# Whole-load squares and sums, one root per store, and paired adds for the last loads in an Lp-pool kernel

## The chip, the cores and the metric

One core of one Trainium2 chip. The metric is the device time of one execution in microseconds (us); profiles are of one execution each. ACT (ScalarE) and DVE (VectorE) are the two engines that compute here; DMA engines move the data, and SPq and ACTq in the profiles are the two queues on which transfers are issued. A transfer "lands" when its last byte is in place.

## The reference

Pooling over windows of four neighbours with p = 2: the root of the mean of squares.

```python
x: (32, 256, 4096) float32;  p = 2.0;  kernel_size = 4
for i in range(1024):
    window = np.abs(x[:, :, 4*i:4*i+4]) ** p
    result[:, :, i] = np.mean(window, axis=-1) ** (1.0 / p)
```

It reads 134.2 MB and writes 33.6 MB, and each input is used once.

## The kernel before

The input is taken as one flat array, cut into 22 loads: 18 of 128 x 13184, then four smaller. Three input slots rotate; results of two loads ("group") gather in one output tile and leave with one store. A load is worked on in pieces (`chunks`): ACT squares the piece in place, DVE sums each four neighbours, ACT takes the root of the piece before it.

```python
    W, O_W = 13184, 6592
    X_SLOTS, O_SLOTS = 3, 2
    slots = [[(W, [4416, 4384, 4384])]] * 18
    slots += [[(6592, [3296, 3296])] * 2, [(6592, [3296, 3296]), (5056, [2528, 2528])]]
    groups = [2] * 9 + [3, 1]
    late = {7, 8, 9, 10}          # groups whose store goes out on the load queue, at the end
    in_x = {9, 10}                # groups whose results lie in an input slot
    # ... (pools, addresses)
    def root(g, o, ends):
        nc.scalar.activation(out=o, in_=o, func=Act.Sqrt, scale=1.0 / k)
        if ends and g not in late:
            store(g, nc.scalar)
    # ...
    for i in range(n):
        s, _, w, chunks = loads[i]
        while ahead < n and loads[ahead][0] < s + X_SLOTS:
            load(ahead)           # nc.sync.dma_start; waits until the slot's last sum is done
            ahead += 1
        # ... (output tile of the group)
        for step in chunks:
            v = xs[i][:, c:c + step]
            nc.scalar.activation(out=v, in_=v, func=Act.Square)
            o = ots[g][:, at + c // k:at + (c + step) // k]
            nc.vector.tensor_reduce(out=o, in_=v.rearrange("p (n j) -> p n j", j=k),
                                    axis=mybir.AxisListType.X, op=mybir.AluOpType.add)
            if pending is not None:
                root(*pending)
            c += step
            pending = (g, o, i == firsts[g] + groups[g] - 1 and c == w)
    root(*pending)
    for g in sorted(late):
        store(g, nc.sync)
```

Of the kernel before, what the change touches and what calls it, by code (L numbers as in the profile page):

```python
# [1 line left out]

# [4 lines left out]


@with_exitstack
def kernel(  # L10
    ctx: ExitStack,
    tc: tile.TileContext,
    x: bass.AP,
    p: float,
    kernel_size: int,
    out: bass.AP,
):






    nc = tc.nc

    assert float(p) == 2.0, "kernel specialized for p == 2"
    k = int(kernel_size)
    assert k == 4, "kernel specialized for kernel_size == 4"

    P = nc.NUM_PARTITIONS  # L30
    fp32 = mybir.dt.float32
    Act = mybir.ActivationFunctionType
    xf = x.rearrange("b c l -> (b c l)")
    of = out.rearrange("b c l -> (b c l)")
    total = xf.shape[0] // P

    W, O_W = 13184, 6592
    X_SLOTS, O_SLOTS = 3, 2
    slots = [[(W, [4416, 4384, 4384])]] * 18
    slots += [[(6592, [3296, 3296])] * 2, [(6592, [3296, 3296]), (5056, [2528, 2528])]]  # L40
    groups = [2] * 9 + [3, 1]
    late = {7, 8, 9, 10}
    in_x = {9, 10}


    loads = [(s, sum(w for w, _ in slot[:j]), *slot[j]) for s, slot in enumerate(slots)
             for j in range(len(slot))]
    n = len(loads)
    assert sum(w for _, _, w, _ in loads) == total

    firsts = [sum(groups[:g]) for g in range(len(groups))]
    assert sum(groups) == n
    group_of = [g for g, count in enumerate(groups) for _ in range(count)]
    columns = [sum(w for _, _, w, _ in loads[firsts[g]:firsts[g] + groups[g]])
               for g in range(len(groups))]

    x_pool = ctx.enter_context(tc.tile_pool(name="x_pool", bufs=X_SLOTS))
    o_pool = ctx.enter_context(tc.tile_pool(name="o_pool", bufs=O_SLOTS))
    ctx.enter_context(tc.manual_schedule())

    def block(flat, g, div):
        at, width = sum(columns[:g]) * P // div, columns[g] * P // div
        return flat[at:at + width].rearrange("(p w) -> p w", p=P)

    slot_tiles = {}
    xs = {}

    def load(i):
        s, at, w, _ = loads[i]
        if at == 0:  # L70
            slot_tiles[s] = x_pool.tile([P, W], fp32, name="xt")
        v = slot_tiles[s][:, at:at + w]
        g = group_of[i]
        src = sum(loads[j][2] for j in range(firsts[g], i))
        nc.sync.dma_start(out=v, in_=block(xf, g, 1)[:, src:src + w])  # L75
        xs[i] = v

    ots = {}

    def store(g, queue):  # L80
        queue.dma_start(out=block(of, g, k), in_=ots[g])  # L81

    def root(g, o, ends):
        nc.scalar.activation(out=o, in_=o, func=Act.Sqrt, scale=1.0 / k)  # L84
        if ends and g not in late:
            store(g, nc.scalar)

    ahead = 0
    while ahead < n and loads[ahead][0] < X_SLOTS - 1:
        load(ahead)  # L90
        ahead += 1
    pending = None
    for i in range(n):
        s, _, w, chunks = loads[i]
        while ahead < n and loads[ahead][0] < s + X_SLOTS:
            load(ahead)
            ahead += 1
        g = group_of[i]
        if i == firsts[g]:
            pool, width = (o_pool, O_W) if g not in in_x else (x_pool, W)  # L100
            t = pool.tile([P, width], fp32, name="ot" if g not in in_x else "xt")
            ots[g] = t[:, 0:columns[g] // k]
        at = sum(loads[j][2] for j in range(firsts[g], i)) // k
        assert sum(chunks) == w
        c = 0
        for step in chunks:
            v = xs[i][:, c:c + step]
            nc.scalar.activation(out=v, in_=v, func=Act.Square)  # L108
            o = ots[g][:, at + c // k:at + (c + step) // k]
            nc.vector.tensor_reduce(  # L110
                out=o, in_=v.rearrange("p (n j) -> p n j", j=k),
                axis=mybir.AxisListType.X, op=mybir.AluOpType.add,
            )
            if pending is not None:
                root(*pending)
            c += step
            pending = (g, o, i == firsts[g] + groups[g] - 1 and c == w)
    root(*pending)
    for g in sorted(late):
        store(g, nc.sync)  # L120


# [1 line left out]
_INS = ['x', 'p', 'kernel_size']  # L124
_OUTS = [((32, 256, 1024), 'float32')]

_NUMBERS = {'p': 2.0, 'kernel_size': 4}


# [26 lines left out]
```

## Time and profile before

| | before |
|---|---|
| median of three runs | 394.89 us (394.77 to 394.97) |
| span of the profiled run | 393.0 us |
| moved | 167.8 MB, 427 GB/s over the span |
| busy, DVE and ACT | 282.4 and 292.4 us |

These lines are from the page of the profile: busy time, and then the span in 40 slices of 9.8 us each, a digit being tenths of busy time.

```profile
DVE 282.4 (72%) x62; ACT 292.4 (74%) x126; POOL 0.2 (0%) x4
...
DMA  8999999999999999999999999999999999999997
GB/s 344 429 429 440 429 424 381 443 459 429 413 440 435 429 427 432 429 440 441 437 448 421 432 462 435 392 429 472 429 413 451 425 429 429 424 429 427 438 429 329
```

No engine that computes is near its limit, and the DMA row has a 9 in every slice but the first and the last. That row is the first thing to look at: where it never falls, the time is bytes over rate.

The groups of instructions by shape (line, engine, operation, shapes, count, then busy us and mean ns of one, then the idle time before it):

```profile
L110 DVE TENSOR_REDUCE ot<-xt 128x1096 f32<-128x4384 f32 x36 | 169.9, 4719 | 6.7 <-ACT xt L108 6.4
L108 ACT ACTIVATE xt<-xt 128x4384 f32<-128x4384 f32 x36 | 138.3, 3843 | 2.9 <-ACT ot L84 2.9
...
L84 ACT ACTIVATE ot<-ot 128x1096 f32<-128x1096 f32 x36 | 39.7, 1103 | 1.1 <-DVE ot L110 0.9
```

The DMA issues, with the median time from issue to landing as the last number:

```profile
xt<-in_x_dram SPq DMA_DIRECT2D x18, 6592.0 KB, 39.7
out_dram<-ot ACTq DMA_DIRECT2D x7, 3296.0 KB, 26.4
...
out_dram<-xt SPq DMA_DIRECT2D x1, 632.0 KB, 5.0
```

A load is under way for 39.7 us although it needs 15.6 us alone: it mostly waits in a queue that is never empty. The end of the timeline (start, duration, engine, what):

```profile
381.39 6.11 SPq L81 DMA_DIRECT2D out_dram<-xt  x2
383.47 0.71 ACT L84 ACTIVATE xt<-xt 128x632 f32<-128x632 f32 x1
383.60 2.79 DVE L110 TENSOR_REDUCE xt<-xt 128x632 f32<-128x2528 f32 x1 [0.46 <-ACT xt L108]
386.42 0.73 ACT L84 ACTIVATE xt<-xt 128x632 f32<-128x632 f32 x1 [2.23 <-DVE xt L110]
```

The last root ends at 387.15 us and the last store leaves with it.

### The profile page before, as it was taken

The page shows a single profiled execution, that of the slowest core. Times are in us where ns is not written, and L with a number is a line of the kernel's source. Part 1 is how long each engine was busy: PE and PEld are TensorE (multiplying, and loading weights), DVE is VectorE, ACT ScalarE, POOL GpSimd, SP SyncE. Part 2 cuts the span into 40 slices and gives each one's busy share as a digit, 9 for nine tenths or more (in the row PEclk, how much of TensorE's full clock was granted, in tenths as well). Part 3 has the DMA queues.
Part 4 walks back from the last instruction along what each step waited for, and adds up shares of the span by engine and source line. Part 5 has one row for each costly group of instructions (what it writes and reads, how often), then busy time and mean ns, then how long its engine had stood idle before and what let it go on. Part 6 is the DMA issues. An engine that isn't in the chain of part 4 may idle for free.

```text
span 393.0 us, 316 instructions
## 1 busy us (share of the span) xinstructions
DVE 282.4 (72%) x62; ACT 292.4 (74%) x126; POOL 0.2 (0%) x4
## 2 busy tenths in 40 slices
DVE  0068989494959495949594959595859686899992
ACT  1099986777786768686958695959595949899991
POOL 0000000000000000000000000000000000000000
DMA  8999999999999999999999999999999999999997
GB/s 344 429 429 440 429 424 381 443 459 429 413 440 435 429 427 432 429 440 441 437 448 421 432 462 435 392 429 472 429 413 451 425 429 429 424 429 427 438 429 329
DMA packets 4754, 167.79 MB, mean 427 GB/s; under 512 B 528, under 2 KB 528, under 8 KB 656
## 3 DMA queue, kind: packets, MB, share of 16 engines
q1 hardware_dynamic: 3744, 144.15, 85.3%
q10 hardware_dynamic: 1008, 23.63, 14.0%
q14 instruction: 2, 0.02, 0.0%
HBM read 134.22 MB, written 33.55 MB: 427 GB/s over the span
## 4 chain that ended last, share of the span: by engine, by line
DMA 62%; ACT 19%; DVE 14%; issue 2%; ACTq 0%; SPq 0%
DMA xt<-in_x_dram 62%; ACT xt L108 15%; DVE ot L110 11%; DVE xt L110 3%; ACT ot L84 3%; ACT xt L84 1%; ACTq L81 0%; SPq L75 0%; ACTq L108 0%
## 5 line engine op out<-in xcount | busy, mean ns | idle before, releaser
L110 DVE TENSOR_REDUCE ot<-xt 128x1096 f32<-128x4384 f32 (+1 forms) x54 | 255.4, 4731 | 102.7 <-ACT xt L108 102.4
L108 ACT ACTIVATE xt<-xt 128x4384 f32<-128x4384 f32 (+3 forms) x62 | 230.3, 3716 | 89.2 <-DMA xt<-in_x_dram 86.3
L84 ACT ACTIVATE ot<-ot 128x1096 f32<-128x1096 f32 (+1 forms) x54 | 59.8, 1108 | 1.8 <-DVE ot L110 0.9
L110 DVE TENSOR_REDUCE xt<-xt 128x824 f32<-128x3296 f32 (+1 forms) x8 | 27.0, 3384 | 1.3 <-ACT xt L108 1.2
L84 ACT ACTIVATE xt<-xt 128x824 f32<-128x824 f32 (+1 forms) x8 | 6.7, 841 | 3.0 <-DVE xt L110 2.9
L108 ACT ACT_TABLE_LOAD x1 | 1.3, 1283 | 0.7 <-PEq L137 0.7
L84 ACT ACT_TABLE_LOAD x1 | 1.3, 1283 | 0.0
L137 POOL MEMSET const-bfloat16-1.0<- 128x1 bf16 x1 | 0.1, 101 | 0.0
L137 POOL MEMSET const-uint8-127<- 128x1 uint8 x1 | 0.1, 101 | 0.0
L137 POOL MEMSET const-float32-0.0<- 128x1 f32 x1 | 0.1, 98 | 0.2 <-issue 0.2
L137 POOL MEMSET const-float32-1.0<- 128x1 f32 x1 | 0.1, 98 | 0.0
## 6 DMA issues: line engine op xcount, KB each, us to landing
xt<-in_x_dram SPq DMA_DIRECT2D x18, 6592.0 KB, 39.7
out_dram<-ot ACTq DMA_DIRECT2D x7, 3296.0 KB, 26.4
xt<-in_x_dram SPq DMA_DIRECT2D x3, 3296.0 KB, 24.6
out_dram<-ot SPq DMA_DIRECT2D x2, 3296.0 KB, 29.6
xt<-in_x_dram SPq DMA_DIRECT2D x1, 2528.0 KB, 26.4
out_dram<-xt SPq DMA_DIRECT2D x1, 2472.0 KB, 9.3
out_dram<-xt SPq DMA_DIRECT2D x1, 632.0 KB, 5.0
```

Of the source, the lines that this page charges most:

```text
L84: nc.scalar.activation(out=o, in_=o, func=Act.Sqrt, scale=1.0 / k)
L108: nc.scalar.activation(out=v, in_=v, func=Act.Square)
L110: nc.vector.tensor_reduce(out=o, in_=v.rearrange("p (n j) -> p n j", j=k), axis=mybir.AxisListType.X, op=mybir.AluOpType.add,)
L137: nc = _bacc.Bacc("TRN2", target_bir_lowering=False, num_devices=1)
```

## The change

Its intent is fewer and larger instructions: one square and one sum per 13184-column load, one root per store. For the last loads, where DVE sets the pace, a sum becomes two adds: the first adds columns 0, 1 of each window to columns 2, 3 and packs its results into the front half of the same tile, the second adds the two that remain. Tiles are fixed in place of rotating pools.

```diff
-    slots = [[(W, [4416, 4384, 4384])]] * 18
-    slots += [[(6592, [3296, 3296])] * 2, [(6592, [3296, 3296]), (5056, [2528, 2528])]]
+    slots = [[(W, [W])]] * 16 + [[(W, [6592, 6592])]] * 2
+    slots += [[(6592, [6592]), (6592, [6592])], [(6592, [6592]), (5056, [2528, 2528])]]
-    in_x = {9, 10}
+    in_x = {9: (2, 0), 10: (2, 4944)}
+    FINE, ENDS, LAG = {21}, {19, 20}, 1
+    PAIRS = 17
...
+    x_tiles = [x_pool.tile([P, W], fp32, name=f"xt{j}") for j in range(X_SLOTS)]
+    o_tiles = [o_pool.tile([P, O_W], fp32, name=f"ot{j}") for j in range(O_SLOTS)]
...
+    def total_sum(o, v, i):
+        if i < PAIRS:
+            nc.vector.tensor_reduce(...)          # as before
+            return
+        q = v.rearrange("p (n j) -> p n j", j=k)
+        front = v[:, 0:v.shape[1] // 2]
+        h = front.rearrange("p (n j) -> p n j", j=2)
+        nc.vector.tensor_tensor(out=h, in0=q[:, :, 0:2], in1=q[:, :, 2:4], op=add)
+        nc.vector.tensor_tensor(out=o, in0=h[:, :, 0], in1=h[:, :, 1], op=add)
...
-            if pending is not None:
-                root(*pending)
+            while pending and pending[0][0] <= done - LAG:
+                root(*pending.pop(0)[1:])
...
+            ends = summed == columns[g] // k
+            if ends or i in FINE or (i in ENDS and c == w):
+                pending.append((done - 1, g, ots[g][:, rooted:summed], ends))
+                rooted = summed
```

More of the change, by code (lines that the diff above doesn't have):

```diff
@@ L55 @@
                for g in range(len(groups))]
-    x_pool = ctx.enter_context(tc.tile_pool(name="x_pool", bufs=X_SLOTS))
-    o_pool = ctx.enter_context(tc.tile_pool(name="o_pool", bufs=O_SLOTS))
+    x_pool = ctx.enter_context(tc.tile_pool(name="x_pool", bufs=1))
+    o_pool = ctx.enter_context(tc.tile_pool(name="o_pool", bufs=1))
+    x_tiles = [x_pool.tile([P, W], fp32, name=f"xt{j}") for j in range(X_SLOTS)]
+    o_tiles = [o_pool.tile([P, O_W], fp32, name=f"ot{j}") for j in range(O_SLOTS)]
     ctx.enter_context(tc.manual_schedule())
@@ L63, in block @@
         return flat[at:at + width].rearrange("(p w) -> p w", p=P)
-    slot_tiles = {}
     xs = {}
@@ L69, in load @@
         s, at, w, _ = loads[i]
-        if at == 0:
-            slot_tiles[s] = x_pool.tile([P, W], fp32, name="xt")
-        v = slot_tiles[s][:, at:at + w]
+        v = x_tiles[s % X_SLOTS][:, at:at + w]
         g = group_of[i]
@@ L86, in root @@
             store(g, nc.scalar)
+    def total_sum(o, v, i):
+        add = mybir.AluOpType.add
+        if i < PAIRS:
+            nc.vector.tensor_reduce(
+                out=o, in_=v.rearrange("p (n j) -> p n j", j=k),
+                axis=mybir.AxisListType.X, op=add,
+            )
+            return
[4 more added lines that the diff above has]
+        nc.vector.tensor_tensor(out=o, in0=h[:, :, 0], in1=h[:, :, 1], op=add)
     ahead = 0
@@ L91 @@
         ahead += 1
-    pending = None
+    pending = []
+    done = 0
     for i in range(n):
@@ L99 @@
         if i == firsts[g]:
-            pool, width = (o_pool, O_W) if g not in in_x else (x_pool, W)
-            t = pool.tile([P, width], fp32, name="ot" if g not in in_x else "xt")
-            ots[g] = t[:, 0:columns[g] // k]
-        at = sum(loads[j][2] for j in range(firsts[g], i)) // k
+            t, first = (o_tiles[g % O_SLOTS], 0) if g not in in_x else (x_tiles[in_x[g][0]], in_x[g][1])
+            ots[g] = t[:, first:first + columns[g] // k]
+            summed = rooted = 0
         assert sum(chunks) == w
@@ L108 @@
             nc.scalar.activation(out=v, in_=v, func=Act.Square)
-            o = ots[g][:, at + c // k:at + (c + step) // k]
-            nc.vector.tensor_reduce(
-                out=o, in_=v.rearrange("p (n j) -> p n j", j=k),
-                axis=mybir.AxisListType.X, op=mybir.AluOpType.add,
-            )
-            if pending is not None:
-                root(*pending)
-            c += step
-            pending = (g, o, i == firsts[g] + groups[g] - 1 and c == w)
-    root(*pending)
+            total_sum(ots[g][:, summed:summed + step // k], v, i)
+            while pending and pending[0][0] <= done - LAG:
+                root(*pending.pop(0)[1:])
+            done += 1
+            c += step
+            summed += step // k
+            ends = summed == columns[g] // k
+            if ends or i in FINE or (i in ENDS and c == w):
+                pending.append((done - 1, g, ots[g][:, rooted:summed], ends))
+                rooted = summed
+    for job in pending:
+        root(*job[1:])
     for g in sorted(late):
```

## The prediction

> **What bounds the kernel now.** The DMA engines. In the page's slices the DMA row is 9 from the second slice to the last but one, 427 GB/s over the span. In the chain of waits the same square recurs every 117 us (50.70, 168.26, 285.00 us), in which six loads of 6.75 MB and three stores of 3.375 MB move: 432 GB/s. The Trainium skill ("DMA: Bandwidth & Descriptors", Specifications) gives 435 GB/s as the fabric ceiling; this trace agrees. All 167.8 MB at 432 GB/s take 388.4 us; with some 1.7 us before the first packet and 1.5 us after the last, that is nearly the span of 393.0 us. DVE is busy 72%, ACT 74%. The compute in the chain only frees slots for loads that then wait in the queue (39.7 us from issue to landing, where a load alone takes 15.6 us). Even the last 20 us move 400 to 450 GB/s until 388 us, so the tail's compute hides under stores.
>
> **What the change does.** The same 22 loads and 11 stores, sizes and queues. 62 squares become 25; 62 sums become 18 reductions and 7 pairs of adds; 62 roots become 13. From the groups by shape, a square costs 180 ns + 0.836 ns per column, a reduction 140 + 1.045, a root 200 + 0.825. ACT's busy time falls from 292 to about 283 us. A 6592-column pair of adds should cost 3.6 + 1.9 us against 7.0 for one reduction ("VectorE: DVE Perf Modes", perf-mode tier table: fp32 tensor_tensor at 1×; no run shows it yet); DVE falls from 282 to about 268 us. None of this is on the critical path.
>
> Latency gets worse. A load is squared in 11.2 us, then reduced in 13.9: the slot comes free 25 us after landing, not 18.7. Loads are issued 6 us later; issue to landing shrinks from 39.7 to about 33 us. A load needs 15.7 to 19.5 us of transfer, so 13 us of queue are left and the engines never run dry. Stores on ACT leave about 12 us later (a whole square and a 5.7 us root ahead); a store lands in some 26 us, about 7 us before its output tile is written again.
>
> Tail, worked through with these durations: group 8's root ends near 365 us (before 359), group 9's store leaves near 383 (381.4), the last near 388.5 (387.2). The queue holds group 8's store until about 385 and group 9's until about 390, so a few tenths to one us is lost.
>
> **Prediction.** 395.1 us, range 393.9 to 396.6. Faster by over 2%: 0.005; within 2%: 0.97; slower by over 2%: 0.025.
>
> **What would show it.** DMA row at 9 throughout, 425 to 428 GB/s; ACT instructions from 126 to 40; 13184-column square 11.2 us, reduction 13.9; adds 3.6 and 1.9; load issue to landing 31 to 35 us; last store issued at 388 to 389 us.
>
> **What would make it wrong.** Strided adds at two cycles an element would put over 20 us more DVE work into a tail where DVE is busiest: the last stores come late, and the kernel ends 10 to 20 us later. A store that lands later than 33 us would hold up the sum two groups on. If 13 us of queue were too little for sixteen drifting engines, the rate in the middle would fall below 425 GB/s.

## The result, and the profile after

Ratios here are the mean time of one kernel's fast runs over that of the other's of the same rounds, so not quite the ratio of the medians quoted.

| | before | after |
|---|---|---|
| median of six runs | 394.92 us (394.77 to 395.22) | 395.84 us (395.61 to 396.42) |
| ratio, 95% interval | | 1.0025 (1.0012 to 1.0038) |
| span of the profiled run | 393.0 us | 393.7 us |
| busy, DVE and ACT | 282.4, 292.4 us | 267.8, 281.7 us |
| median us from issue to landing, full load | 39.7 | 31.7 |

The kernel is a quarter of a per cent slower, outside the noise but far below anything that 86 fewer ACT instructions might have suggested. The page of after:

```profile
DVE 267.8 (68%) x32; ACT 281.7 (72%) x40; POOL 0.2 (0%) x4
...
DMA  8999999999999999999899999999999999999996
GB/s 343 429 429 429 434 455 439 386 429 429 434 469 434 442 445 383 431 471 429 386 429 471 429 426 439 421 429 429 429 445 442 426 450 450 402 429 425 438 423 291
```

The same row of nines (one 8 in the middle). ACT and DVE lost 10.7 and 14.6 us of work, and nobody was waiting for it. The groups by shape show what each new instruction costs:

```profile
L93 DVE TENSOR_REDUCE ot<-xt 128x3296 f32<-128x13184 f32 x16 | 222.2, 13886 | 105.1 <-ACT xt L125 105.1
L125 ACT ACTIVATE xt<-xt 128x13184 f32<-128x13184 f32 x16 | 179.0, 11190 | 91.8 <-DMA xt<-in_x_dram 90.1 <-ACT ot L86 1.7
L86 ACT ACTIVATE ot<-ot 128x6592 f32<-128x6592 f32 x9 | 51.2, 5684 | 0.4 <-DVE ot L103 0.4
...
L102 DVE TENSOR_TENSOR xt<-xt 128x3296 f32<-128x3296 f32 x5 | 17.9, 3587 | 6.0 <-ACT xt L125 5.9
L93 DVE TENSOR_REDUCE ot<-xt 128x1648 f32<-128x6592 f32 x2 | 14.0, 7020 | 5.5 <-ACT xt L125 3.7 <-DMA out_dram<-ot 1.9
L103 DVE TENSOR_TENSOR xt<-xt 128x1648 f32<-128x1648 f32 x3 | 5.6, 1875 | 0.1
```

A pair of adds over 6592 columns takes 3.59 + 1.88 = 5.46 us, one reduction of the same 7.02 us. That is what the prediction had put down for adds at full pace, though they read with strides and the first writes into the tile it reads; no run has the same adds without strides. The issues:

```profile
xt<-in_x_dram SPq DMA_DIRECT2D x18, 6592.0 KB, 31.7
out_dram<-ot ACTq DMA_DIRECT2D x7, 3296.0 KB, 27.2
...
out_dram<-xt SPq DMA_DIRECT2D x1, 632.0 KB, 5.9
```

The 8 us between 39.7 and 31.7 have two parts. From the fourth load to the last full one, a load is issued 3.0 to 6.8 us later than before, and it lands between 4.7 us sooner and 0.7 us later than before (the stores, which share the engines, now leave later). So the later issue did not make the loads land late: only the wait in the queue shrank. The end of the timeline:

```profile
381.72 5.65 SPq L83 DMA_DIRECT2D out_dram<-xt  x2
383.80 0.71 ACT L86 ACTIVATE xt<-xt 128x632 f32<-128x632 f32 x1
383.93 1.48 DVE L102 TENSOR_TENSOR xt<-xt 128x1264 f32<-128x1264 f32 x1 [1.61 <-ACT xt L125]
385.44 0.82 DVE L103 TENSOR_TENSOR xt<-xt 128x632 f32<-128x632 f32 x1
386.29 0.73 ACT L86 ACTIVATE xt<-xt 128x632 f32<-128x632 f32 x1 [1.77 <-DVE xt L103]
```

The last root ends at 387.02 us, 0.13 us *earlier* than before, yet the last store lands 5.9 us after its issue, not 5.0. That is the whole of the 0.7 us between the two spans, and it is lost neither by ACT nor by DVE.

It can be traced one step further. Each transfer is done by sixteen DMA engines, and the trace has sixteen landing events for each ("DMA: Bandwidth & Descriptors" in the Trainium skill, section "Why a DMA increments its semaphore by 16 and not by 1", says that each engine's last descriptor counts one; the trace agrees). The sixteen landings of the last load, in us after the first of them, worked out from the trace:

```
before   0.0 0.0 0.0 0.0 0.2 0.2 0.3 0.3 0.3 0.3 0.4 0.4 0.4 0.6 0.8 0.9
after    0.0 0.0 0.1 0.1 0.2 0.2 0.2 0.3 0.3 0.3 0.4 0.5 0.5 0.5 0.6 1.9
```

In after, one engine is 1.3 us behind the fifteenth, and one is still so far behind at the last store: 0.96 us of spread before, 1.98 after. The kernel ends when the last engine does. (A landing does not name its engine; that it is the same one is inferred from the lag, which is 1.3 us in each transfer that lands from 340.4 us on.) The lag arises in the body of the kernel: it is 0.5 us in the first four loads, 0.9 us in the next, which lands at 87.6 us and is the first to share its way with a store, and 1.4 us in the load that lands at 184.7 us.

The packet records of the traces (start, time and size of each packet; no view prints them) tell what the sixteen did on the whole. The packets of loads and stores took 389.8 us per engine in before and 389.6 us in after, and from 5 to 383 us at least sixteen were in flight at over 99% of the moments in both. So the engines of after had no more to do and did not stand idle; the time only fell less evenly on them.

### The profile page after: what moved, and what is told of

It is laid out like the page before. It is cut to its first block, busy times and chain, and to the rows that moved or that the text cites. A ratio compares the mean times of both kernels' runs of the same rounds, so it can differ in the third digit from the quotient of the medians.

```text
span 393.7 us, 192 instructions
## 1 busy us (share of the span) xinstructions
DVE 267.8 (68%) x32; ACT 281.7 (72%) x40; POOL 0.2 (0%) x4
## 2 busy tenths in 40 slices
DMA packets 4752, 167.77 MB, mean 426 GB/s; under 512 B 528, under 2 KB 528, under 8 KB 656
## 3 DMA queue, kind: packets, MB, share of 16 engines
q10 hardware_dynamic: 1008, 23.63, 13.9%
## 4 chain that ended last, share of the span: by engine, by line
DMA 47%; ACT 26%; DVE 19%; issue 6%; SPq 0%; ACTq 0%
DMA xt<-in_x_dram 47%; ACT xt L125 19%; DVE ot L93 14%; ACT ot L86 6%; DVE xt L102 3%; DVE ot L103 1%; DVE xt L103 1%; ACT xt L86 1%; ACT L86 0%; SPq L77 0%; ACTq L83 0%
## 5 line engine op out<-in xcount | busy, mean ns | idle before, releaser
L93 DVE TENSOR_REDUCE ot<-xt 128x3296 f32<-128x13184 f32 (+1 forms) x18 | 236.2, 13123 | 110.6 <-ACT xt L125 108.7
L125 ACT ACTIVATE xt<-xt 128x13184 f32<-128x13184 f32 (+2 forms) x25 | 223.1, 8936 | 102.0 <-DMA xt<-in_x_dram 100.3
L86 ACT ACTIVATE ot<-ot 128x6592 f32<-128x6592 f32 x9 | 51.2, 5684 | 0.4 <-DVE ot L103 0.4
L102 DVE TENSOR_TENSOR xt<-xt 128x3296 f32<-128x3296 f32 (+1 forms) x7 | 20.9, 2983 | 7.6 <-ACT xt L125 7.5
L86 ACT ACTIVATE xt<-xt 128x632 f32<-128x632 f32 (+2 forms) x4 | 6.0, 1492 | 2.2 <-DVE xt L103 2.2
L103 DVE TENSOR_TENSOR xt<-xt 128x1648 f32<-128x1648 f32 (+1 forms) x5 | 7.3, 1452 | 0.2
L103 DVE TENSOR_TENSOR ot<-xt 128x1648 f32<-128x1648 f32 x2 | 3.7, 1874 | 0.1
L125 ACT ACT_TABLE_LOAD x1 | 1.3, 1283 | 0.7 <-PEq L156 0.7
L86 ACT ACT_TABLE_LOAD x1 | 1.3, 1283 | 0.0
## 6 DMA issues: line engine op xcount, KB each, us to landing
xt<-in_x_dram SPq DMA_DIRECT2D x18, 6592.0 KB, 31.7
```

The source lines that it names most:

```text
L102: nc.vector.tensor_tensor(out=h, in0=q[:, :, 0:2], in1=q[:, :, 2:4], op=add)
L103: nc.vector.tensor_tensor(out=o, in0=h[:, :, 0], in1=h[:, :, 1], op=add)
```

## The experiments

All diffs are against after unless it is said otherwise, and are cut to changed lines. Kernels of one call ran on one chip beside before (394.94, 394.94 and 394.84 us in the three calls), and each ratio is to the before of its own call. "Spread" is the time from the first to the last of the sixteen landings of the last load.

### Is compute anywhere on the path? `dma_only`

```diff
+    BIT = 128
+    for t in o_tiles: nc.vector.memset(t, 1.0)
-            v = xs[i][:, c:c + step]
+            v = xs[i][:, c:c + BIT]            # squares, sums and roots likewise: 128 columns, 32 results
```

> Wrong result on purpose: after, but every square, sum and root works on 128 columns (32 results) only; all loads and stores keep their sizes, queues and order. If compute is wholly off the critical path, as predicted: 393.3 to 395 us, at most 0.4% under before, with DVE and ACT busy under 15%. If compute still holds up the DMA anywhere: 391 us or less.

Measured: 395.06 us (394.66 to 395.39), ratio to before 1.0004 (0.9992 to 1.0017), result wrong as intended. That is 0.06 us above the range expected for compute off the path. The page:

```profile
DVE 19.0 (5%) x34; ACT 11.8 (3%) x40; POOL 0.2 (0%) x4
...
DMA  8999999999999999999999999999999999999997
```

With DVE and ACT down from 549.5 us of work together to 30.8, the time is the same within noise. This settles the main question: with these transfers, taking away nearly all of the squares, sums and roots gains nothing that can be measured (the interval reaches 0.08% below before). What the change saved lay beside the critical path.

### Which part brought the 0.9 us? `fixed_only`, `coarse_body`, `coarse_tail`

Two theories stood against each other. A: one of the sixteen DMA engines falls behind in the body (loads 0 to 15), because stores leave later there and mix with loads. B: the loss comes from the new tail (the last six loads). A third cause could be the fixed tiles, so that comes first.

`fixed_only` keeps the fixed tiles and takes back everything else:

```diff
-    slots = [[(W, [W])]] * 16 + [[(W, [6592, 6592])]] * 2
-    slots += [[(6592, [6592]), (6592, [6592])], [(6592, [6592]), (5056, [2528, 2528])]]
+    slots = [[(W, [4416, 4384, 4384])]] * 18
+    slots += [[(6592, [3296, 3296])] * 2, [(6592, [3296, 3296]), (5056, [2528, 2528])]]
-    FINE, ENDS, LAG = {21}, {19, 20}, 1
-    PAIRS = 17
+    FINE, ENDS, LAG = set(range(22)), set(), 1
+    PAIRS = 99
```

> Before's pieces of squares, sums and roots, but the fixed tiles of after. Both theories: same as before, 394.9 us (394.6 to 395.3), because the tiles change neither the order of the DMA nor any size. If it takes 395.6 or more, the 0.9 us of the change comes from the tiles and not from the coarse pieces.

Measured: 394.79 us, ratio 0.9998 (0.9985 to 1.0010). The tiles do nothing.

`coarse_body` has whole-load pieces for loads 0 to 15 and before's pieces and reductions after that:

```diff
-    slots = [[(W, [W])]] * 16 + [[(W, [6592, 6592])]] * 2
-    slots += [[(6592, [6592]), (6592, [6592])], [(6592, [6592]), (5056, [2528, 2528])]]
+    slots = [[(W, [W])]] * 16 + [[(W, [4416, 4384, 4384])]] * 2
+    slots += [[(6592, [3296, 3296])] * 2, [(6592, [3296, 3296]), (5056, [2528, 2528])]]
-    FINE, ENDS, LAG = {21}, {19, 20}, 1
-    PAIRS = 17
+    FINE, ENDS, LAG = set(range(16, 22)), set(), 1
+    PAIRS = 99
```

> After's coarse pieces for loads 0 to 15, before's pieces for the last six loads. Theory A (the 0.9 us is one DMA engine of the sixteen that falls behind the others while late stores and loads interleave in the body; it is still behind at the end): 395.5 to 396.3 us, and the 16 landings of the last store spread over about 2 us, as after, not 1 us as before. Theory B (the 0.9 us comes from the new tail: adds, one long root of group 8, fewer pieces): 394.7 to 395.2 us.

Measured: 396.01 us, ratio 1.0027 (1.0013 to 1.0041). The time hits theory A, but the run is not clean: its last store left only at 389.6 us, so the spread at that store was 0.2 us, not 2; at the last load it was 1.79 us. It needed a repeat with a quicker tail (`body_adds` below).

`coarse_tail` is the other half:

```diff
-    slots = [[(W, [W])]] * 16 + [[(W, [6592, 6592])]] * 2
+    slots = [[(W, [4416, 4384, 4384])]] * 16 + [[(W, [6592, 6592])]] * 2
-    FINE, ENDS, LAG = {21}, {19, 20}, 1
+    FINE, ENDS, LAG = set(range(16)) | {21}, {19, 20}, 1
```

> Before's pieces for loads 0 to 15, after's pieces and adds for the last six loads. Theory A: 394.7 to 395.2 us, landings of the last store spread over about 1 us. Theory B: 395.5 to 396.3 us.

Measured: 394.99 us, ratio 1.0001 (0.9989 to 1.0014), spread 1.63 us. The new tail costs nothing; theory B falls. The spread was larger than the 1 us expected, so spread is not as tidy as theory A had it.

### What do the adds pay for? `no_adds`

```diff
-    PAIRS = 17
+    PAIRS = 99
```

> After with the two adds of the last five loads put back to one reduction each, coarse pieces kept. Worked through with 7.02 us a reduction in place of 5.46 for the pair: DVE then sets the tail, group 8's root ends near 366.5, group 9's store leaves near 388 (after: 381.7) and the last store near 393.7 (387.1); the queue is empty from about 385.5 until then, so the kernel ends near 400 us (398 to 402). If the tail hides under the queued stores whatever DVE takes: 396 us.

Measured: 399.51 us (398.7 to 400.5), ratio 1.0119 (1.0104 to 1.0134). The last store left at 393.1 us and the stretches of the tail show the hole (us, busy DVE, ACT and POOL with counts, clock, DMA share, GB/s):

```profile
380.00:384.00 4.00, 4.00 (x1) 3.90 (x2) 0.00 (x0) 1.00 0.70 303
384.00:386.00 2.00, 2.00 (x2) 0.32 (x1) 0.00 (x0) 1.00 0.00 0
386.00:388.00 2.00, 2.00 (x1) 2.00 (x2) 0.00 (x0) 1.00 0.00 0
388.00:390.00 2.00, 0.85 (x2) 2.00 (x2) 0.00 (x0) 1.00 1.12 475
```

So the coarse pieces do have a price in the tail: there DVE works flat out, and with whole-load pieces it starts on the last loads too late. The adds buy back 1.2% less 0.25%, close to 1% (399.51 - 395.84 = 3.7 us, medians). The two parts of the change belong together: coarse pieces without adds lose, and before's tail was on time without adds.

### What did the third slot pay for? `two_fine`, `two_coarse`

Loads rotate over two tiles; the third only holds the last outputs. `two_fine` applies this to `fixed_only`, `two_coarse` to after.

```diff
+    LOAD_SLOTS = 2
-        v = x_tiles[s % X_SLOTS][:, at:at + w]
+        v = x_tiles[s % LOAD_SLOTS][:, at:at + w]
-    while ahead < n and loads[ahead][0] < X_SLOTS - 1:
+    while ahead < n and loads[ahead][0] < LOAD_SLOTS - 1:
-        while ahead < n and loads[ahead][0] < s + X_SLOTS:
+        while ahead < n and loads[ahead][0] < s + LOAD_SLOTS:
```

> Before's pieces, fixed tiles, loads rotating over two tiles in place of three (the third only holds the last outputs). A slot is held 18.4 us after landing, a load takes 15.7 us alone and about 2.5 us of latency: 36.6 us a slot without stores in the way, just under the 39 us that two loads and a store take of the DMA engines. So nearly DMA-bound, some idle: 400 to 425 us.

> After with loads rotating over two tiles in place of three. Theory (the longer hold of the slot costs nothing only because the third slot pays for it): a slot is held 25.1 us, so a cycle is at least 43.3 us for two loads without stores in the way, up to 51 with; 430 to 490 us, 5 to 15% over the same change in fine pieces. If the coarse pieces were free for another reason, such as fewer waits, no slower than the fine pieces in two tiles.

Measured: `two_fine` 432.71 us, ratio 1.0957 (1.0941 to 1.0973), slower than I expected. `two_coarse` 445.09 us, ratio 1.1262 (1.1238 to 1.1285), in its range, but only 2.9% over the fine pieces. From the chains of waits, `two_fine` first:

```profile
207.71 3.89 ACT xt L126
211.62 4.76 DVE ot L94
217.53 3.76 ACT xt L126
221.31 4.73 DVE ot L94
226.06 25.15 DMA xt<-in_x_dram
251.24 3.89 ACT xt L126
```

and `two_coarse`:

```profile
212.71 11.20 ACT xt L126
223.90 0.02 issue
223.93 13.90 DVE ot L94
237.84 18.49 DMA xt<-in_x_dram
256.36 11.20 ACT xt L126
```

One of the slot's cycles is 251.24 - 207.71 = 43.5 us in fine pieces and 256.36 - 212.71 = 43.65 us in coarse. Hold plus transfer is 18.3 + 25.2 in the one and 25.1 + 18.5 in the other. With fine pieces the store and the other load are in a load's way, so it takes 25 us and not the 15.7 I had reckoned with; with coarse pieces it is nearly alone. My estimate of the fine form left out that the transfer itself lengthens. These cycles are nearly equal, so they do not account for the 12 us between the two times. Over half of it comes in the last cycle of the full loads, where no store is in the way. `two_fine`, and under it `two_coarse`:

```profile
337.02 3.89 ACT xt L126
...
355.37 18.33 DMA xt<-in_x_dram
373.78 3.89 ACT xt L126
```

```profile
343.47 11.20 ACT xt L126
...
387.18 7.93 ACT xt L126 x2
```

There the fine cycle is 373.78 - 337.02 = 36.8 us, as I had reckoned (36.6), and the coarse one 387.18 - 343.47 = 43.7 us: 6.9 us more, about the 6.8 us by which the slot is held longer. What stands: once slots are short, hold time is on the path in both, and the longer hold of after (25.1 us for 18.3) shows in full where no store lengthens the fine form's transfer; with three slots it was paid out of the wait in the queue.

### What spreads the sixteen engines? `sp_stores`, `body_adds`, `fine_late`, `half_loads`

Theory A said: two queues interleave, and one engine falls behind. (The Trainium skill, same page, section "Queues, rings and completion order", says that each DMA engine takes turns between the queues that have work, packet by packet. The packet records of after agree: put into sixteen chains by ends and starts, 784 of the 896 packets of stores on ACT's queue are followed by a packet of a load.) Then one queue should cure it.

```diff
-            store(g, nc.scalar)
+            store(g, nc.sync)
```

> After with all stores issued on the load queue, so that no second queue interleaves with loads. Theory A (one engine falls behind where two queues interleave): the landings of the last store spread over about 1.1 us, as those of the first load do, and the time returns to 394.6 to 395.3 us. If the engines drift for another reason: still about 2 us of spread and 395.6 to 396.4 us. Rival: stores wait behind two loads, land late and hold up the sums two groups on: over 398 us.

Measured: 397.04 us (396.93 to 397.51), ratio 1.0059 (1.0046 to 1.0072), and the spread grew from 1.1 us at the first load to 2.97 us at the last. The time lies above the second range and below the third. The cause named in theory A falls: the engines drift apart without a second queue, and further. The link between spread and time holds.

`body_adds` is `coarse_body` with `PAIRS = 16`, so that its tail is on time:

> The coarse body with before's pieces in the tail, as in coarse_body, but the last six loads summed by adds. coarse_body took its 396.0 us with its last store leaving at 389.6 us, so it did not test the body alone: its tail was late. With adds the last store should leave by 387 us. Theory A, mended (coarse pieces in the body leave the sixteen engines further apart, for whatever reason): 395.4 to 396.3 us, spread 1.6 to 2.6 us. Rival (coarse_body was slow only by its late tail, and after by something in its own tail): 394.7 to 395.2 us, spread about 1 to 1.6 us.

Measured: 395.81 us, ratio 1.0025 (1.0012 to 1.0039); last store at 387.6 us, 0.6 us later than expected; spread 2.15 us. With `coarse_tail`: the coarse body alone brings the whole 0.25%, the tail none.

`fine_late` is `fixed_only` with stores that leave later:

```diff
-            while pending and pending[0][0] <= done - LAG:
+            while pending and pending[0][0] <= done - (3 if i < 16 else 1):
```

> Before's pieces, fixed tiles, but in the body each root waits for two squares more, so each store leaves some 10 us later into the loads, as in after. If the later stores are what spreads the engines: 395.4 to 396.3 us and a spread near 2 us. If it is the size of the pieces or the time at which loads are issued: as fixed_only, 394.6 to 395.1 us and a spread of 1 to 1.6 us.

Measured: 396.74 us (396.33 to 397.42), ratio 1.0050 (1.0037 to 1.0062). The stores left at 65.15, 103.80, 143.56 us and so on (`fixed_only` 55.38, 94.95, 133.89; after 68.95, 104.45, 145.43). The spread was 2.96 us, against 1.40 in `fixed_only`. Its last store also left late, at 389.9 us, so its time is not clean; but the spread was there at the last load, before that. Small pieces with late stores spread the engines as after does, and more. So the size of the instructions is not needed for it. Whether late stores alone are enough is not separated: loads were issued some 2 us later too (37.7 us from issue to landing against 39.7), and this is one profile.

`half_loads`:

```diff
-        nc.sync.dma_start(out=v, in_=block(xf, g, 1)[:, src:src + w])
+        cut = [0, w // 2, w] if w == W else [0, w]
+        for a, b in zip(cut, cut[1:]):
+            nc.sync.dma_start(out=v[:, a:b], in_=block(xf, g, 1)[:, src + a:src + b])
```

> After with each 13184-column load issued as two of 6592, so that one row of a load is 26 KB and not 53 KB. If engines fall apart by rows, the unit in which two queues take turns: the spread halves to about 1 us, 394.7 to 395.3 us. If they lose time at each border between transfers, of which there are now more: spread over 2.5 us, 396.5 us or more.

Measured: 395.80 us, ratio 1.0022 (1.0010 to 1.0035). The spread did halve, to 0.92 us, but the time did not return: the span less the spread rose to 392.7 us, about 0.9 us more than elsewhere. Half of the expectation was right. What was lost in its place is in the packet records: a row of 53 KB took 1947 ns in after, and each of its two halves 978 ns here (medians), 9 ns more for the row, or 1.3 us over the 144 rows that an engine has; the packets took 390.9 us per engine against 389.6.

### The control, `after_again`

> After once more, as the control for this call: 395.6 to 396.4 us. Earlier traces: span less the spread of the last store's 16 landings is 391.6 to 392.0 us in six kernels, whatever the compute does. If that holds, this one has a spread of 1.6 to 2.6 us and a span of 391.6 to 392.0 plus it.

Measured: 395.67 us (395.06 to 395.88), ratio 1.0017 (1.0004 to 1.0029); the profiled run was the quickest of the five, with a span of 393.0 us and a spread of 1.55 us (1.60 at the last store). Span less the latter is 391.4, a little under the 391.6 expected.

### Spread and span side by side

| kernel | span | spread at the last load | span less spread |
|---|---|---|---|
| before | 393.0 | 0.92 | 392.1 |
| fixed_only | 393.2 | 1.40 | 391.8 |
| dma_only | 393.1 | 1.44 | 391.7 |
| coarse_tail | 393.3 | 1.63 | 391.7 |
| after_again | 393.0 | 1.55 | 391.5 |
| coarse_body | 393.4 | 1.79 | 391.6 |
| after | 393.7 | 1.91 | 391.8 |
| body_adds | 394.0 | 2.15 | 391.8 |
| fine_late | 394.9 | 2.96 | 391.9 |
| sp_stores | 394.8 | 2.97 | 391.9 |
| half_loads | 393.6 | 0.92 | 392.7 |
| no_adds | 396.9 | 1.85 | 395.1 |

In ten of the twelve kernels the last column is 391.5 to 392.1 us, while the spread goes from 0.9 to 3.0. `no_adds` stands out because its queue ran dry for over 4 us, `half_loads` because its packets took longer. The spread is not tied to late stores line by line: `coarse_tail`, with its first store at 55.56 us as in before, has more of it than `after_again`, with its first at 68.60 us, and `half_loads`, with its first at 68.71 us, has no more than before. Each line is one profile, so this is a match over twelve kernels and not a proof.

## Why the prediction was right

- **The bound.** "The DMA engines": right. `dma_only` shows it: 395.06 us with DVE and ACT busy 5% and 3%.
- **The costs.** A 13184-column square was put at 11.2 us and measured 11.19, the reduction at 13.9 and measured 13.89, the adds at 3.6 and 1.9 and measured 3.59 and 1.87. DVE at 268 and measured 267.8, ACT at 283 and measured 281.7. Durations of the small forms, fitted as a fixed part and a part per column, held at three times the width.
- **The slack.** "Loads are issued 6 us later": measured 3.0 to 6.8. Issue to landing was put at 33 us (31 to 35), measured 31.7. "The engines never run dry": right, shown by the DMA row (9 but for one 8 between its ends) and by the packets in flight.
- **The stores.** "About 12 us later": measured 9 to 13 us. "About 7 us before its output tile is written again": wrong for the last store on ACT. Loads 16 and 17 are worked in halves, so their first sum comes 5.5 us sooner than I had it, and DVE waited 1.9 us for that store ("DMA out_dram<-ot 1.9" in the reductions' line above). It cost nothing in the end.
- **The size.** 395.1 us predicted in a range of 393.9 to 396.6, measured 395.84.
- **The tail, where the reasoning was wrong.** "The last near 388.5 (387.2) ... so a few tenths to one us is lost." The last store left at 387.04 us, earlier than before. The loss was about the size named, 0.9 us, but not for that reason, so that agreement is luck: it comes from the body (`body_adds` has it, `coarse_tail` has not), and in the traces it lies in DMA engines that finish behind the rest. In the profile of after that is one engine; in `after_again` four of the sixteen landings come about 1.0 to 1.5 us after the first. The step that failed is the sum of the tail: I had the last store late by 1.3 us and the engines in step. The sum was off from its start: group 8's root, put at 365 us, ended at 363.4.

What stays open is why the engines drift. A second queue is not needed for it (`sp_stores`), nor are large instructions (`fine_late`). That the later stores of after are what spreads its engines is argued from these two, not shown: no run has after's pieces with early stores, `fine_late` shifted its loads too, and the table has exceptions. Which engine it is, and in which packets it loses its time, was not worked out.

## What to carry to other kernels

When the DMA row is at 9 from end to end and the bytes can't shrink, remove the compute in a test kernel before tuning it: here one such run said that all tuning of ACT and DVE could bring nothing that can be measured. Larger instructions save fixed costs and lengthen the time for which a buffer is held; here that was free with three slots, where loads waited in a queue, and cost time with two, so look at the time from issue to landing, and look at the tail by itself, where there is no queue left to pay from. A difference of a quarter of a per cent, as here, can come from DMA engines that finish apart, and the instruction counts did not explain it.

## What the Trainium skill lacked or had wrong

- "SBUF — State Buffer", summary of rules for kernel authors, says to estimate HBM to SBUF transfers at about 358 GB/s. That would make this kernel 469 us (167.77 MB over 358 GB/s); it ran at 427 GB/s over the span. "HBM Reference", section "Specifications (TRN2)", has the better figure for a core streaming alone, about 425.
- "ScalarE: Activation LUTs", section "What ACT_TABLE_LOAD costs", gives 1283 ns and a drain of about 1380 ns for a switch. The load took 1283 ns here too, but the switch from squares to roots cost no more than that: in after it started at 61.93 us, 0.02 us after the square, and the root started at 63.22 us.
- No page says how far apart the sixteen DMA engines end in a stream of loads and stores: 0.9 to 3.0 us between the first and the last of them at the last load, in twelve kernels with the same bytes, and the end of the kernel follows the last one.
- No page has a measured duration for a `tensor_reduce` along each partition's row in fp32: a fit to the groups by shape gives 140 ns + 1.045 ns per input column, from 2528 to 13184 columns.
